# Hybrid encoder layer: first loads on two queues, both halves of the first norm together, first group's stacks without transfers, priority for copies of projection banks

## The chip, the cores and the metric

The kernel runs on one core of a Trainium2 chip. The metric is the device time of one execution in microseconds. The times of the kernel before are 1128.06, 1128.92 and 1130.89; their median, 1128.92, is the time before. The profile is of one further execution that took 1127.34.

The engines are TensorE (PE; its weight loads are PEld), VectorE (DVE), ScalarE (ACT), GpSimd (POOL) and SyncE (SP). SP and ACT issue the transfers of this kernel. A queue works its instructions in order: an instruction that waits holds all behind it on its engine.

## The reference

One encoder layer on x of 1024 tokens by 1024 channels, float32. An RMS norm feeds one projection of 2304 columns that belong to two token mixers: window attention with 8 query heads in two groups (each group of 4 shares one key and one value head, |i-j| <= 128, a sink logit per head, rotary positions on the first 16 of 64 channels), and neighbourhood attention with 8 heads on a 16 x 64 grid. Their outputs get a norm each and go through one output projection; a gated MLP of width 2816 with a convolution of width 3, and a last norm, follow.

```python
hn = rmsnorm(h, norm_mix[l])
proj = jnp.einsum('bsd,de->bse', hn, w_in[l])
qa, ka, va, qb, kb, vb = jnp.split(proj, splits, axis=-1)
qa = partial_rope(qa.reshape(B, S, A_HEADS, HEAD_DIM), cos, sin)
ka = partial_rope(ka.reshape(B, S, A_KV_HEADS, HEAD_DIM), cos, sin)
o_a = window_gqa_sink(qa, ka, va, sink[l])
o_b = neighbourhood_attention(...)
mix = jnp.concatenate([rmsnorm(o_a, norm_a[l]), rmsnorm(o_b, norm_b[l])], axis=-1)
h = h + jnp.einsum('bse,ed->bsd', mix, w_out[l])
...
h = h + conv_gated_mlp(hn, w_gate[l], w_up[l], conv_w[l], conv_b[l], w_down[l])
return rmsnorm(h, norm_final)
```

## The kernel before

Activations are held transposed: tiles of 128 channels by 1024 tokens (`S`), worked in two halves of 512 (`h`). Each float32 operand of a matmul is split in a high part (ACT, a copy to fp32r) and a low part (DVE, the difference), and a product is three matmuls: high by high, high by low, low by high (`block`, L112 to L115). One such step of three, for one 128-channel slice `k` and one half, is called a block below.

**Order.** PE's order is as written (`manual_schedule`, L91). The other engines' orders are made at build time by a scheduler that takes what is ready by priority; `tc.high_priority(offset=...)` raises the priority of what it encloses. Tiles come from pools with a fixed number of buffers by tag: `raw` 2, `whi` and `wlo` 3 each, the `s` banks of PSUM 2.

**Start (L508 to L572).** SP issues all loads: the parameters, the first half of x tile 0, the first 128 channels of the weights of projection tiles 0 and 1, the second half of x tile 0, the rest of those weights' first four slices, then x tiles 1 to 3, the weights' second halves, and x tiles 4 to 7. x tile 0 is split by halves (`first_x`), the others whole (`split_scaled`, L123). Projection tiles m = 0 (a key and a value head), 1 and 2 (two query heads each) belong to attention group 0, m = 3 to 5 to group 1, m = 6 to 17 to the grid attention. Tiles 0 and 1 run through k = 0 to 7 together as x arrives (L566 to L571). Beside it the squares of x are summed (`squares`, L135).

**First norm (L580 to L598).** The third tile's first half runs, then for each half of the tokens in turn: sums of the squares by matmuls of one column (`ss`, `inverse_narrow`, L145), a square root on ACT and a reciprocal on DVE, and a broadcast by four matmuls (`sw`, `widen`, L157), which ACT copies to `rstd1`. Then the banks of tiles 0 and 1 are copied out with the scale (`evacuate`, L168), and the third tile's second half runs, with the posts of tiles 0 and 1 among its blocks.

**Posts (L244).** `rotate` (L178) moves the rotary rows of a tile to a folded layout by two transfers issued by ACT (`f<-t`, L186), turns them in four DVE operations, and moves them back by two transfers issued by SP (`t<-f`, L192). There are two folded buffers. `split_pair` (L194) then makes from a tile of two query heads the two stacked operands `q` (high part of a head in one half of the partitions, low part in the other) by one ACT copy, one DVE operation and three transfers issued by SP (L200 to L202); `split_k` (L217) does the same for a key head with one copy, one difference and two transfers. `split_v` (L227) transposes the values on PE (`vt`).

**After that** `fill(n)` runs n blocks of the further projections and output products (`rest`, L616), each projection tile `Project.run` (L452) being 16 blocks in `pj` banks with a copy by `evacuate` after each half. `settle` (L605) calls the post of a finished tile once `LAG` blocks of the next have run. First come `FILL0` = 26 blocks; then six score steps (L710; each two matmuls into an `s` bank, L273, followed by the masked minimum `p<-s` on DVE, L295, and the exponential on ACT, L299); then `FILL1` = 12 blocks; then the units of attention, between whose steps blocks are run at `RATES`. The first two score steps use the query stacks of tile 1, the next two those of tile 2.

Of the kernel before, what the change touches and what calls it, by code (L numbers as in the profile page):

```python
# [30 lines left out]

LAG = 3
FILL0, FILL1 = 26, 12
RATES = [40, 49, 21, 21, 21, 21, 13, 19, 20, 17]
SPARE = (3, 6)
# [16 lines left out]
def hybrid_layer(tc, xT, w_in, w_out, w_gate, w_up, w_down, small, sink, rpb, consts, rope, out):  # L52
    nc = tc.nc
    with ExitStack() as ctx:
# [32 lines left out]
        cst = cpool.tile([128, K_END], F32, name="cst")  # L87
        ident = cst[:, K_ID:K_ID + 128]


# [72 lines left out]

        def inverse_rms_wide(sq, dim, tag):
            return widen(inverse_narrow([sq], dim, tag), tag)


# [10 lines left out]
        def rotate(t, n):  # L178

            m = slice(0, n)  # L180
            f, u = folded[0]
            folded.append(folded.pop(0))
            rows = lambda s: t[4 * s:n:8].rearrange("a (c w) -> a c w", w=128)
            fold = lambda s: f[m, s]
            for s in range(2):
                nc.scalar.dma_start(fold(s), rows(s))  # L186
            for s in range(2):
                nc.vector.tensor_tensor(u[m, s], f[m, 1 - s], rs[m, s], op=ALU.mult)
            nc.vector.tensor_tensor(f[m], f[m], rc[m], op=ALU.mult)
            nc.vector.tensor_tensor(f[m], f[m], u[m], op=ALU.add)  # L190
            for s in range(2):
                nc.sync.dma_start(rows(s), fold(s))  # L192

        def split_pair(t):  # L194
# [7 lines left out]
            nc.sync.dma_start(f32(a[64:128, :]), t[0:64])  # L202
            return [a, b]

        def split_qk(t):
# [239 lines left out]
        class Project:  # L445
# [64 lines left out]
        xg, first = [None] * KT, [Project(0), Project(1)]  # L510
        xts, sqs = [], []

        def load_x(k):
            xt = big("xt", "op")
            nc.sync.dma_start(xt, xT[k])
            xts.append(xt)


        xt0 = big("xt", "op")
        xts.append(xt0)  # L520
        head = [[wpool.tile([128, 4, 128], dt, name="w0", tag=tag, bufs=n) for dt, tag, n in ((F32, "raw", 2), (F32R, "whi", 3), (F32R, "wlo", 3))] for _ in first]
        nc.sync.dma_start(xt0[:, 0:HALF], xT[0, :, 0:HALF])
        for p, (raw, _, _) in zip(first, head):
            nc.sync.dma_start(raw[:, 0:1], w_in[p.m, :, 0:1, :])
        nc.sync.dma_start(xt0[:, HALF:S], xT[0, :, HALF:S])
        for p, (raw, _, _) in zip(first, head):
            nc.sync.dma_start(raw[:, 1:4], w_in[p.m, :, 1:4, :])
        xg[0] = big("xgh", "xg", F32R), big("xgl", "xg", F32R)
        g0 = col(C_NMIX)

        def first_x(h):
            nc.scalar.activation(xg[0][0][:, tsl(h)], xt0[:, tsl(h)], AF.Copy, scale=g0)
            nc.vector.scalar_tensor_tensor(xg[0][1][:, tsl(h)], xt0[:, tsl(h)], g0, f32(xg[0][0][:, tsl(h)]), op0=ALU.mult, op1=ALU.subtract)

# [11 lines left out]
        for k in range(1, 4):  # L546
            load_x(k)
        for p in first:
            p.w += load_w(w_in[p.m, :, 4:8, :])
        for k in range(4, KT):  # L550
            load_x(k)
        nc.sync.dma_start(cst, consts)
# [6 lines left out]
        nc.sync.dma_start(turns[:, 0:2], rope)  # L559
        for _ in range(2):  # L560
            t = quarters(big("f", "mix"))
            folded.append((t[:, 0], t[:, 1]))

        banks = [[bank("pj", "pj") for _ in range(2)], [bank("o", "o") for _ in range(2)]]
        acc = None
        for k in range(KT):  # L566
            if k:
                xg[k] = split_scaled(xts[k], col(C_NMIX + k), "xg", "xg")
# [784 lines left out]
```

## Time and profile before

| | |
|---|---|
| times of three runs | 1128.06, 1128.92, 1130.89 us |
| the profiled execution | 1127.34 us |
| its span | 1125.6 us |
| mean granted clock of PE | 0.984 |
| transfers | 147.03 MB |

The span runs from the first to the last instruction of the trace; the execution's own time is 1.7 us longer. In the page's first part each engine stands with its busy time, its share of the span and its instructions. A row of the waits reads: engine, operation and line, who ended the wait, total, times, longest. A row of the timeline reads: start, duration, engine, line, operation, output and inputs, shape, and in brackets the idle time before it and what ended that. The duration of an instruction that follows another closely overlaps with its neighbour's; the step from start to start is then shorter.

### The profile page before, as it was taken

The page shows a single profiled execution, that of the slowest core. Times are in us where ns is not written, and L with a number is a line of the kernel's source. Part 1 is how long each engine was busy: PE and PEld are TensorE (multiplying, and loading weights), DVE is VectorE, ACT ScalarE, POOL GpSimd, SP SyncE. Part 2 cuts the span into 40 slices and gives each one's busy share as a digit, 9 for nine tenths or more (in the row PEclk, how much of TensorE's full clock was granted, in tenths as well). Part 3 has the DMA queues.
Part 4 walks back from the last instruction along what each step waited for, and adds up shares of the span by engine and source line. Part 5 has one row for each costly group of instructions (what it writes and reads, how often), then busy time and mean ns, then how long its engine had stood idle before and what let it go on. Part 6 is the DMA issues. An engine that isn't in the chain of part 4 may idle for free.

```text
span 1125.6 us, 14912 instructions
## 1 busy us (share of the span) xinstructions
PE 1086.2 (96%) x5124; PEld 903.0 (80%) x5124; DVE 852.4 (76%) x1549; ACT 548.3 (49%) x1033; POOL 105.7 (9%) x186
## 2 busy tenths in 40 slices
PE   8969999999999999999999999999999999999995
PEld 6858888888878877888788888888888878888884
DVE  6557888766689666989988778877877868797843
ACT  7235767655667433445434334334343645543531
POOL 0212332233223100000000000000000000000001
PEclk8989999999999999999999999999999999999997
DMA  7253220333215316412443223222322799875823
GB/s 266 65 122 80 53 57 29 84 92 87 75 31 148 103 47 211 163 47 78 166 160 122 105 92 123 102 103 94 122 103 94 244 302 294 268 221 174 272 83 144
DMA packets 67708, 147.03 MB, mean 131 GB/s; under 512 B 8112, under 2 KB 16816, under 8 KB 67632
## 3 DMA queue, kind: packets, MB, share of 16 engines
q1 hardware_dynamic: 57552, 121.04, 34.6%
q10 hardware_dynamic: 10080, 25.04, 5.9%
q8 instruction: 40, 0.66, 0.2%
q14 instruction: 36, 0.29, 0.1%
HBM read 103.58 MB, written 28.57 MB: 117 GB/s over the span
## 4 chain that ended last, share of the span: by engine, by line
PE 86%; DVE 7%; DMA 3%; ACT 2%; issue 2%; SPq 0%; POOLq 0%; ACTq 0%; DVEq 0%
PE pj L113 7%; PE pj L114 7%; PE pj L115 7%; PE dn L797 6%; PE dn L799 6%; PE dn L798 6%; PE z L799 5%; PE z L797 5%; PE z L798 5%; PE x L797 3%; PE x L799 3%; PE x L798 3%; PE s L273 3%; PE y L799 3%; PE y L797 3%; PE y L798 3%
## 5 line engine op out<-in xcount | busy, mean ns | idle before, releaser
L797 PE MATMUL dn<-xd,whi 128*128 128x512 f32 x308 | 120.2, 390 | 1.1 <-ACT c L1218 1.1
L786 ACT ACTIVATE whi<-ws 128x512 fp32r<-128x512 f32 (+1 forms) x100 | 60.1, 622 | 123.9 <-DVE ws L903 76.3
L799 PE MATMUL dn<-xd,wlo 128*128 128x512 f32 x308 | 119.8, 389 | 0.0
L798 PE MATMUL dn<-xd,whi 128*128 128x512 f32 x308 | 119.8, 389 | 0.0
L799 PE MATMUL z<-hg,wlo 128*128 128x512 f32 x264 | 103.1, 390 | 0.7 <-DVE wlo L787 0.7
L113 PE MATMUL pj<-xgh,whi 128*128 128x512 f32 x248 | 103.4, 417 | 0.0
L797 PE MATMUL z<-hg,whi 128*128 128x512 f32 x264 | 102.9, 390 | 0.0
L798 PE MATMUL z<-hg,whi 128*128 128x512 f32 x264 | 102.7, 389 | 0.0
L299 ACT ACTIVATE p<-p,nm 128x385 f32<-128x385 f32 (+3 forms) x128 | 75.1, 586 | 56.3 <-DVE nm L295 52.3
L115 PE MATMUL pj<-xgh,wlo 128*128 128x512 f32 x248 | 97.7, 394 | 0.0
L114 PE MATMUL pj<-xgl,whi 128*128 128x512 f32 x248 | 97.5, 393 | 0.0
L303 POOL TENSOR_SCALAR p<-p,sm 128x384 f32<-128x384 f32 (+1 forms) x128 | 73.5, 588 | 237.3 <-DVE sm L301 218.2
L787 DVE TENSOR_TENSOR wlo<-raw,whi 128x512 fp32r<-128x512 f32 (+1 forms) x102 | 66.3, 669 | 22.7 <-ACT whi L786 22.5
L787 DVE TENSOR_TENSOR wlo<-ws,whi 128x512 fp32r<-128x512 f32 (+1 forms) x100 | 66.7, 681 | 19.5 <-ACT whi L786 19.5
L309 DVE TENSOR_TENSOR pl<-pt,ph 128x384 fp32r<-128x384 f32 (+2 forms) x108 | 63.1, 588 | 23.2 <-ACT ph L308 22.1
L786 ACT ACTIVATE whi<-raw 128x512 fp32r<-128x512 f32 (+1 forms) x102 | 60.4, 611 | 41.4 <-DMA raw<-in_w_down_dram 18.4
L1108 ACT ACTIVATE xd<-xd 128x512 fp32r<-128x512 f32 x77 | 47.3, 627 | 58.0 <-DMA xd<-x 56.5
L308 ACT ACTIVATE ph<-pt 128x384 fp32r<-128x384 f32 (+2 forms) x108 | 55.3, 514 | 38.2 <-PE pt L408 30.8
L1209 POOL TENSOR_TENSOR y<-y,wide 128x512 f32<-128x512 f32 x4 | 5.1, 1283 | 727.0 <-ACT y L1208 727.0
L799 PE MATMUL y<-hg,wlo 128*128 128x512 f32 x176 | 68.7, 390 | 0.5 <-DVE wlo L787 0.5
L797 PE MATMUL x<-hg,whi 128*128 128x512 f32 x176 | 68.7, 390 | 0.0
L799 PE MATMUL x<-hg,wlo 128*128 128x512 f32 x176 | 68.5, 389 | 0.0
(199 smaller groups left out, 2657.8 us busy)
## 6 DMA issues: line engine op xcount, KB each, us to landing
xd<-x SPq DMA_DIRECT2D x77, 256.0 KB, 5.1
raw<-in_w_down_dram SPq DMA_DIRECT2D x72, 256.0 KB, 3.4
raw<-in_w_gate_dram SPq DMA_DIRECT2D x22, 512.0 KB, 3.5
raw<-in_w_up_dram SPq DMA_DIRECT2D x22, 512.0 KB, 4.0
x<-c ACTq DMA_DIRECT2D x22, 512.0 KB
raw<-in_w_in_dram SPq DMA_DIRECT2D x32, 256.0 KB, 3.2
raw<-in_w_down_dram SPq DMA_DIRECT2D x36, 192.0 KB, 3.8
x<-t ACTq DMA_DIRECT2D x11, 512.0 KB, 2.6
```

The costliest lines, as they stand in the source:

```text
L113: nc.tensor.matmul(ps, w[0], x[0][:, tsl(h)], start=first, stop=False)
L114: nc.tensor.matmul(ps, w[0], x[1][:, tsl(h)], start=False, stop=False)
L115: nc.tensor.matmul(ps, w[1], x[0][:, tsl(h)], start=False, stop=last)
L299: nc.scalar.activation(p[:, j, 0:e], p[:, j, 0:e], AF.Exp, bias=nm, scale=-1.0, accum_out=sm[:, j:j + 1])
L303: nc.gpsimd.tensor_scalar(p[:, i, 0:m], p[:, i, 0:m], sm[:, i:i + 1], 1.0, op0=ALU.mult, op1=ALU.mult)
L308: nc.scalar.activation(ph[:, 0:n], ps[:, 0:n], AF.Copy)
L309: nc.vector.tensor_tensor(pl[:, 0:n], ps[:, 0:n], f32(ph[:, 0:n]), op=ALU.subtract)
L786: nc.scalar.activation(hi, src, AF.Copy)
L787: nc.vector.tensor_tensor(lo, src, f32(hi[:, :, :]), op=ALU.subtract)
L797: nc.tensor.matmul(ps, w[0], x[0], start=first and i == 0, stop=False, skip_group_check=True)
L798: nc.tensor.matmul(ps, w[0], x[1], start=False, stop=False, skip_group_check=True)
L799: nc.tensor.matmul(ps, w[1], x[0], start=False, stop=last and i == len(ws) - 1, skip_group_check=True)
```

## The change

- **First loads.** The parameters and the weights of tiles 0 and 1 (first four slices) are issued by ACT, ahead of its first table load. SP begins with x tiles 0 and 1, in halves; x tile 1 is now split by halves too.
- **First norm.** `ss` of both halves, three blocks of the third tile, `sw` of both halves; the other five blocks and then both posts. Those posts, and tile 2's, have a priority offset of 400.
- **Rotation.** The second `f<-t` transfer goes to SP; there is a third folded buffer.
- **First group's stacks.** `split_first` and `split_first_k` write each half of the partitions by an ACT copy and a DVE operation of 64 rows; no transfers. Group 1 keeps `split_pair` and `split_k`.
- **Numbers.** `FILL0` 26 to 22, the first two `RATES` 40, 49 to 43, 50; tile 3 is posted after `LATE` = 13 blocks in place of `LAG` = 3.
- **Bank copies** of the projection tiles (all but the last) have a priority offset of 500.

```diff
-LAG = 3
-FILL0, FILL1 = 26, 12
-RATES = [40, 49, 21, 21, 21, 21, 13, 19, 20, 17]
+LAG, LATE = 3, 13
+FILL0, FILL1 = 22, 12
+RATES = [43, 50, 21, 21, 21, 21, 13, 19, 20, 17]
...
-        nc.sync.dma_start(par[:, 0:C_SINK], small)
+        nc.scalar.dma_start(par[:, 0:C_SINK], small)
...
+        def load_x(k, parts=1):
+            xt = big("xt", "op")
+            n = S // parts
+            for i in range(parts):
+                nc.sync.dma_start(xt[:, i * n:(i + 1) * n], xT[k, :, i * n:(i + 1) * n])
+            return xt
...
+        for ks in (slice(0, 1), slice(1, 4)):
+            for m, (raw, _, _) in enumerate(head):
+                nc.scalar.dma_start(raw[:, ks], w_in[m, :, ks, :])
+        xts = [load_x(0, 2), load_x(1, 2)]
...
             for s in range(2):
-                nc.scalar.dma_start(fold(s), rows(s))
+                (nc.scalar, nc.sync)[s].dma_start(fold(s), rows(s))
...
+        def split_first(t):
+
+            a, b = big("q", "op", F32R), big("q", "op", F32R)
+            for x, hi, lo in ((a, slice(0, 64), slice(64, 128)), (b, slice(64, 128), slice(0, 64))):
+                nc.scalar.activation(x[hi], t[hi], AF.Copy, scale=-HD ** -0.5)
+                nc.vector.scalar_tensor_tensor(x[lo], t[hi], -HD ** -0.5, f32(x[hi, :]), op0=ALU.mult, op1=ALU.subtract)
+            return [a, b]
+
+        def split_first_k(t):
+            a, b = big("ka", "op", F32R), big("kb", "op", F32R)
+            up, down = slice(0, 64), slice(64, 128)
+            nc.scalar.activation(a[up], t[up], AF.Copy)
+            nc.vector.tensor_tensor(b[up], t[up], f32(a[up, :]), op=ALU.subtract)
+            nc.vector.tensor_tensor(a[down], t[up], f32(a[up, :]), op=ALU.subtract)
+            nc.scalar.activation(b[down], t[up], AF.Copy)
+            return a, b
...
-                    ka[g] = split_k(t, 0)
+                    ka[g] = split_k(t, 0) if g else split_first_k(t)
...
-                    qa[g, i - 1] = split_pair(t)
+                    qa[g, i - 1] = split_pair(t) if g else split_first(t)
...
-                        evacuate(self.t, ps, h, self.grid)
+                        with tc.high_priority(offset=500):
+                            evacuate(self.t, ps, h, self.grid)
...
-        first_x(0)
+        for k in range(2):
+            xg[k] = big("xgh", "xg", F32R), big("xgl", "xg", F32R)
+        split_x(0, 0)
         first_w(slice(0, 1))
-        first_x(1)
+        split_x(0, 1)
         first_w(slice(1, 4))
+        for h in range(2):
+            split_x(1, h)
...
-        for _ in range(2):
-            t = quarters(big("f", "mix"))
-            folded.append((t[:, 0], t[:, 1]))
+        t = quarters(big("f", "mix"))
+        folded += [(t[:, 0], t[:, 1]), (t[:, 2], t[:, 3]), (turns[:, 2], turns[:, 3])]
...
+        vs1 = [inverse_narrow([acc[:, tsl(h)]], D, "pt") for h in range(2)]
+        rest3 = product(ps3[1], third.w, xg, 1)
+        for _ in range(3):
+            next(rest3)
         for h in range(2):
-            nc.scalar.activation(rstd1[:, tsl(h)], inverse_rms_wide(acc[:, tsl(h)], D, "pt"), AF.Copy)
+            nc.scalar.activation(rstd1[:, tsl(h)], widen(vs1[h], "pt"), AF.Copy)
...
-        for i, _ in enumerate(product(ps3[1], third.w, xg, 1)):
-            if i == 3:
-                first[0].post()
-            if i == 6:
-                first[1].post()
+        for _ in rest3:
+            pass
+        for p in first:
+            with tc.high_priority(offset=400):
+                p.post()
...
-            while waiting and (len(waiting) > 1 or age >= LAG):
+            while waiting and (len(waiting) > 1 or age >= (LATE if waiting[0].m == 3 else LAG)):
...
-                waiting.pop(0).post()
+                with tc.high_priority(offset=400 if m == 2 else 0):
+                    waiting.pop(0).post()
```

More of the change, by code (lines that the diff above doesn't have):

```diff
@@ L88, in hybrid_layer @@
         ident = cst[:, K_ID:K_ID + 128]
+        def load_x(k, parts=1):
[4 more added lines that the diff above has]
+            return xt
+        head = [[wpool.tile([128, 4, 128], dt, name="w0", tag=tag, bufs=n) for dt, tag, n in ((F32, "raw", 2), (F32R, "whi", 3), (F32R, "wlo", 3))] for _ in range(2)]
+        for ks in (slice(0, 1), slice(1, 4)):
+            for m, (raw, _, _) in enumerate(head):
+                nc.scalar.dma_start(raw[:, ks], w_in[m, :, ks, :])
+        xts = [load_x(0, 2), load_x(1, 2)]
         ctx.enter_context(tc.manual_schedule(engines={mybir.EngineType.PE}))
@@ L162, in widen @@
             return wide
-        def inverse_rms_wide(sq, dim, tag):
-            return widen(inverse_narrow([sq], dim, tag), tag)
         def evacuate(t, ps, h, grid):
@@ L510, in hybrid_layer, with split_x @@
         xg, first = [None] * KT, [Project(0), Project(1)]
[L511 to L533, printed above, removed]
+        def split_x(k, h):
+            g = col(C_NMIX + k)
+            hi, lo = (t[:, tsl(h)] for t in xg[k])
+            nc.scalar.activation(hi, xts[k][:, tsl(h)], AF.Copy, scale=g)
+            nc.vector.scalar_tensor_tensor(lo, xts[k][:, tsl(h)], g, f32(hi), op0=ALU.mult, op1=ALU.subtract)
         def first_w(ks):
@@ L538, in first_w @@
                 nc.vector.tensor_tensor(lo[:, ks], raw[:, ks], f32(hi[:, ks]), op=ALU.subtract)
-        first_x(0)
+        for k in range(2):
+            xg[k] = big("xgh", "xg", F32R), big("xgl", "xg", F32R)
+        split_x(0, 0)
         first_w(slice(0, 1))
-        first_x(1)
+        split_x(0, 1)
         first_w(slice(1, 4))
+        for h in range(2):
+            split_x(1, h)
         for p, (_, hi, lo) in zip(first, head):
             p.w = [(hi[:, j, :], lo[:, j, :]) for j in range(4)]
-        for k in range(1, 4):
-            load_x(k)
+        for k in range(2, 4):
+            xts.append(load_x(k))
         for p in first:
@@ L550, in hybrid_layer @@
         for k in range(4, KT):
-            load_x(k)
+            xts.append(load_x(k))
         nc.sync.dma_start(cst, consts)
@@ L566, in hybrid_layer @@
         for k in range(KT):
-            if k:
+            if k > 1:
                 xg[k] = split_scaled(xts[k], col(C_NMIX + k), "xg", "xg")
```

## The prediction

> **What bounds the kernel now.** I read the page first, then who made PE wait, then PE's busy time in short stretches, then the order of time around the two places where PE loses most.
>
> ```profile
> span 1125.6 us, 14912 instructions
> PE 1086.2 (96%) x5124; PEld 903.0 (80%) x5124; DVE 852.4 (76%) x1549; ACT 548.3 (49%) x1033; POOL 105.7 (9%) x186
> ```
>
> PE is the bound and its order is written by hand, so only time in which PE waits or runs at a lower clock can be won: 39.4 us of idle time, and slow stretches inside the busy time. PE's waits in the first 90 us:
>
> ```profile
> PE s L273 <- DMA q<-t: 8.5, 1, 8.5
> PE pj L113 <- ACT xgh L125: 1.8, 1, 1.8
> ```
>
> The first is the score matmul that waits for the last transfer of `split_pair`; the second is the start, where the second x tile is late. Stretches of 3.41 us show what such a wait costs beside itself (the columns are length, busy time and count of PE, PEld, DVE, ACT, POOL, then granted clock, DMA share, GB/s):
>
> ```profile
> 3.80:7.21 3.41, 2.61 (x12) 1.60 (x11) 1.28 (x4) 2.00 (x5) 0.00 (x0) 1.00 0.86 249
> 7.21:10.62 3.41, 1.84 (x6) 0.94 (x6) 1.65 (x3) 2.33 (x4) 0.00 (x0) 1.00 0.90 344
> 10.62:14.04 3.42, 2.33 (x5) 1.54 (x6) 2.88 (x3) 3.42 (x5) 0.00 (x0) 0.51 0.97 355
> 14.04:17.45 3.41, 3.41 (x10) 2.64 (x9) 3.41 (x4) 3.41 (x5) 0.00 (x0) 0.50 1.00 394
> 68.65:72.06 3.41, 1.40 (x9) 1.04 (x7) 2.34 (x6) 1.62 (x2) 0.00 (x0) 1.00 0.43 96
> 72.06:75.48 3.42, 0.00 (x0) 0.00 (x0) 2.08 (x4) 2.23 (x7) 0.94 (x2) 0.51 0.42 85
> 78.89:82.30 3.41, 3.25 (x11) 2.77 (x11) 2.18 (x9) 1.71 (x7) 0.54 (x2) 0.50 0.31 94
> ```
>
> After a stretch with PE busy 1.84 or 1.40 of 3.41 the granted clock is 0.5, and it returns after one full busy stretch. Each late operand is thus paid a second time. By stage:
>
> ```profile
> 5.12:33.83 28.71, 25.97 (x96) 19.81 (x97) 23.26 (x25) 20.24 (x24) 7.24 (x7) 0.88 0.65 237
> 33.83:39.27 5.44, 5.44 (x25) 4.50 (x24) 1.81 (x3) 1.92 (x2) 0.30 (x1) 1.00 0.51 142
> 39.27:44.37 5.10, 3.78 (x34) 3.63 (x32) 1.92 (x5) 1.12 (x3) 1.58 (x4) 1.00 0.33 101
> 69.42:82.53 13.11, 4.44 (x16) 3.75 (x15) 6.36 (x18) 5.80 (x15) 1.71 (x4) 0.61 0.55 125
> 40.83 1.13 PE L161 MATMUL sw<-cst,v 128*128 128x128 f32 x8 [0.61 <-PE ss L150]
> 43.46 1.16 PE L161 MATMUL sw<-cst,v 128*128 128x128 f32 x8 [0.71 <-DVE v L154]
> ```
>
> At full clock the 24 matmuls of the third tile's first half take 5.44, 0.227 each. The 96 of the first two tiles (5.12 to 33.83) would take 21.8 and take 28.7: **6.9 lost**. The norm loses 0.61 + 0.71 = **1.3**. At the first scores PE waits 8.5 and then runs at half clock until 82.30; the 3.7 us from 78.56 on hold 1.9 of full-clock work: **10.4 lost**. In all 18.6 us lie where the change acts.
>
> **The change, part by part.** T0 is the start of the first `ss` matmul (39.27 now).
>
> *First loads.*
>
> ```profile
> 0.73 1.28 ACT L95 ACT_TABLE_LOAD   x1 [0.73 <-PEq L1342]
> 3.07 0.91 SPq L527 DMA_DIRECT2D w<-in_w_in_dram  x2
> 4.01 1.39 SPq L515 DMA_DIRECT2D xt<-in_xT_dram  x3
> 4.15 0.72 ACT L532 ACTIVATE xgh<-xt,par 128x512 fp32r<-128x512 f32 x1 [1.92 <-DMA xt<-in_xT_dram]
> 6.33 0.72 ACT L532 ACTIVATE xgh<-xt,par 128x512 fp32r<-128x512 f32 x1 [1.06 <-DMA xt<-in_xT_dram]
> 9.98 1.15 ACT L125 ACTIVATE xgh<-xt,par 128x1024 fp32r<-128x1024 f32 x1 [1.08 <-DMA xt<-in_xT_dram]
> 11.03 1.04 ACT L139 ACTIVATE sq<-xt 128x1024 f32<-128x1024 f32 x1
> 22.25 0.63 ACT L108 ACTIVATE whi<-raw 128x512 fp32r<-128x512 f32 x1 [2.65 <-PE pj L114]
> 12.36 1.22 DVE L141 TENSOR_TENSOR sq<-sq 128x1024 f32<-128x1024 f32 x1
> 13.50 1.28 DVE L126 SCALAR_TENSOR_TENSOR xgl<-xt,par,xgh 128x1024 fp32r<-128x1024 f32 x1
> ```
>
> ACT now issues five transfers (0.44 each, half of the 0.91) ahead of its table load: 0.73 + 2.2 + 1.28 + the warm-up 0.2 = 4.4 in place of 4.15, so PE starts 0.2 later. On SP the third and fourth issues are x1's halves (the fourth waits until a first transfer has landed). Its bytes gain less than the 2.4 us by which the issue is earlier, for the engines already show shares of 0.86 and 0.90 from 3.80 on; I take x1's halves at 8.4 and 9.2 instead of 9.98 (bounds: 6.33, where x0's second half is there now, and 9.98). With `split_x` per half (0.65 ACT, then 0.65 DVE) PE waits some 0.9 for k=1, and 0.5 for k=2's low part. Then something new is late: `whi` of tile 1's second weight half reuses the slot of tile 0's first. Now ACT is there early and waits 2.65 for PE. In the changed order it stands behind `xgh` of k=2 to 6, three squares and a `whi`, 5×1.05 + 3×0.95 + 0.5 (the steps of the rows 9.98 and 11.03, neighbours overlapping by 0.1) from x2's landing at 10.7, 0.52 MB at 355 GB/s after x1: 19.3; I add 0.3 for a raw weight that lands late: done at 20.2; PE, no longer slow, wants it at 18.8. With its `wlo` that stops PE 1.85. Start: 0.2 + 0.4 ramp + 0.9 + 0.5 + 1.85 = 3.9 lost in place of 6.9, **T0 = 36.3, gain 3.0**; bounds 0 (the bytes come no earlier, or the new stop costs clock) and 5.4 (only ramp and x1 remain). The third tile's operands and the squares are done by 31 by the same sums; that is cover of 5 us for the norm.
>
> By the Trainium skill ("TensorE: Matmul & The Clock Gate", section Part 1) the clock falls after an idle window of about 3.4 us; by that a stop of 1.85 costs no clock. The row 7.21:10.62 speaks against it: 1.84 busy was low enough. With the page the gain at the start stays 3.0; by the row it is 1.3 (half a stretch less) if the stop lies within one stretch.
>
> *Norm for both halves.* Both `ss`, three blocks, both `sw`, five blocks. The chain from `ss` to `v` needs 0.7 and has 2.0 us of blocks over it: the 1.3 goes, nothing is late.
>
> *Stacks without transfers.*
>
> ```profile
> 46.00 3.15 ACTq L186 DMA_DIRECT2D f<-t  x4
> 48.21 0.28 DVE L188 TENSOR_TENSOR f<-f,turns 64x128 f32<-64x128 f32 x1 [1.64 <-DMA f<-t]
> 51.61 0.41 DVE L189 TENSOR_TENSOR f<-f,turns 128x256 f32<-128x256 f32 x1
> 51.75 2.79 SPq L192 DMA_DIRECT2D t<-f  x4
> 54.58 1.06 ACT L221 ACTIVATE ka<-t 64x1024 fp32r<-64x1024 f32 x1 [4.71 <-DMA t<-f]
> 57.38 0.69 DVE L170 TENSOR_TENSOR t<-pj,rstd 128x512 f32<-128x512 f32 x1
> 59.03 0.63 ACT L108 ACTIVATE whi<-raw 128x512 fp32r<-128x512 f32 x1 [1.67 <-PE pj L114]
> 59.11 1.22 DVE L199 SCALAR_TENSOR_TENSOR t<-t,q 128x1024 fp32r<-128x1024 f32 x1
> 69.85 0.48 DVE L295 CUSTOM_DVE_ANT_0 p<-s,cst,nsink 128x256 f32<-128x256 f32 x1 [0.90 <-PE s L273]
> 74.87 0.55 SPq L202 DMA_DIRECT2D q<-t  x1
> 78.56 0.55 PE L273 MATMUL s<-ka,q 128*128 128x256 f32 x1 [8.51 <-DMA q<-t]
> ```
>
> Eight transfers go, the last issued at 74.87 and waited for until 78.56. Three 64-row ACT copies (1.06) and three DVE operations (1.22) are added; ACT and DVE have room here, but not free: they stand in one row. PE after T0: `ss` 1.9, three blocks 2.0, `sw` 2.0, five blocks 3.4, `vt` 0.8 (moved behind the blocks), third job from T0+10.1; `FILL0` is 22, so the first score comes at T0+25.1. The rotation: tiles out of the banks by T0+10.2, transfers 2.2 (48.21 from 46.00), DVE until T0+15.3, back transfers issued 0.7 apart on SP; all three tiles lie by T0+20. Two queues for `f<-t` save its serial issue. The loads that SP queues behind these transfers are for the job after next; they cost nothing.
>
> In the changed order a `whi` stands ahead of `ka` on ACT, and it waits for twelve blocks of the third job (as at 59.03), T0+18.2. Then `ka`, `kb` and four `q` copies, to T0+24.8. DVE: `kb` and `ka` low parts and one `q` (1.14 each back to back, 13.50 less 12.36), two bank copies (0.61), three `q`, a `wlo`, and the four rotation operations of job m=3 (1.3): 19.9 + 3.4 + 1.2 + 3.4 + 0.6 + 1.3 = T0+29.8. Only then stands the first `p<-s` (0.48). Score matmuls 1 and 2 fill both `s` banks at T0+25.8; the third needs the first bank back: T0+30.4. So **the wait for a transfer becomes one for DVE's queue**: 4.6, then steps 3 to 6 at DVE's pace (0.9 more), end T0+32.1. PE was idle for over half of some stretch, so the clock falls again; I charge 1.0 for what is left of it after T0+32.1 (bounds 0.2 and 1.9). Sum 6.5 in place of 10.4, **gain 3.9**; bounds 1.5 and 9.5 (`p<-s` not held).
>
> *Priority of bank copies, `LATE`, `RATES`.* The four blocks and the `vt` taken out before the scores are done later: no work is saved, and the comparison above counts losses only. m=3's stack is wanted eight units later, so posting it at 13 is free.
>
> ```profile
> 113.00:170.00 57.00, 55.82 (x305) 47.46 (x304) 48.24 (x142) 41.59 (x106) 19.19 (x43) 1.00 0.21 54
> PE vt L233 <- DVE pl L309: 2.5, 3, 1.2
> ```
>
> DVE is 85% busy there and PE loses 1.2 in 57. From 84 to 340 the transposes wait 2.5 for a bank copy that stands behind `pl`; a copy with priority could win that, and one ahead of `pl` or `p<-s` could cost its 0.69. I take +0.2; bounds -3 and +2.
>
> Sum: 3.0 + 1.3 + 3.9 + 0.2 = 8.4 of the profiled execution's 1127.34, which lies 1.6 under the median of 1128.92. Against that median: **1120.5 us**.
>
> **Rivals.**
> 1. *Both new stops are smaller*: x lands sooner, the scheduler's row on DVE runs faster than my sum. For it: PE's own wants are the only late thing. Against: the order on ACT and DVE is fixed. Gains 5.4 + 1.3 + 7.5 (10.4 less 2.9 of pacing and clock) = 14: 1115.
> 2. *The two queues bring no bytes earlier*, so the change doesn't do what it says at the start. For: shares 0.86 and 0.90, and 344 GB/s while x1 is on its way. Against: 249 GB/s before that. Gain 8.4 - 3.0 = 5.4: 1123.5. The Trainium skill ("DMA: Bandwidth & Descriptors", section Issuing engines are not separate DMA queues) says just this: all queues run on the same 16 engines, a second issuer saves issue time alone. Its time is the 1123.5; the early 249 GB/s beside a 0.86 share half agrees.
> 3. *No net change*: start 0, and the DVE row longer by two more operations that PE then waits for: gain 0 to 3, 1127.
> 4. *Slower*: bank copies with priority stand ahead of `pl` and `p<-s` in the stretch where DVE is 85% full. 28 copies at 0.69 are 19 us if PE feels each: 1139. It decides once more than 12 of 28 (8.4/0.69) hit PE. Against: one filler block (0.68) between most steps covers one copy, and in the changed order most moved ahead by one or two places.
>
> **How the numbers follow.** Forecast (1117 to 1123) 0.50; rival 1 0.17; rival 2 0.14; rival 3 0.11; rival 4 0.08. The range 1113 to 1126.5 leaves out rival 4 and part of rival 3. About 0.3%, 3.4 us, is what a measurement can tell from no change: faster 0.81, same 0.11, slower 0.08.
>
> **What would show it.** Start: PE's wait at k=1 under 1 us, clock 1.0 from 10.6 to 17.4, a new wait of `o` for ACT `whi` near 19, `ss` at 35 to 37.5. Norm: no wait before `sw`. Stacks: no `q<-t` transfer before the first scores, and PE waiting 3 to 6 us with DVE `p<-s` named; if it waits under 1, rival 1 holds. After 113: PE's idle time as now; if it grows by over 5 with DVE named, rival 4. I am wrong most likely in the DVE row before the first `p<-s`, or in when x1 lands.

## The result, and the profile after

The changed kernel takes 1118.76 us, the median of seven runs (1115.87 to 1125.44), beside 1128.39 for the kernel before (1128.06 to 1131.67): a ratio of 0.9912, 95% interval 0.9893 to 0.9932. The forecast was 1120.5. The profiled execution took 1115.87 us, the fastest of the seven, with a span of 1114.1 and a mean granted clock of 0.990.

The page of the changed kernel, its first lines:

```profile
span 1114.1 us, 14912 instructions
...
PE 1083.9 (97%) x5124; PEld 902.4 (81%) x5124; DVE 854.2 (77%) x1553; ACT 551.7 (50%) x1037; POOL 109.4 (10%) x186
```

As many instructions as before, and PE's busy time falls by only 2.3 us: what went is time in which PE stood. Where it went is read from three stages: PE's first product to the first `ss` of the first norm (T0); T0 to the end of the sixth score step; from there to the first `ss` of the second norm (`ss<-ones,sqb`, called N2 below). First the changed kernel, then the kernel before (length, busy time and count of PE, PEld, DVE, ACT, POOL, then granted clock, DMA share, GB/s).

```profile
5.47:36.10 30.63, 30.09 (x120) 23.62 (x121) 24.19 (x28) 22.32 (x27) 11.32 (x7) 1.00 0.63 225
36.10:69.22 33.12, 29.38 (x144) 24.30 (x143) 21.66 (x45) 12.14 (x18) 1.91 (x4) 0.95 0.21 63
69.22:392.09 322.87, 315.98 (x1708) 268.46 (x1708) 241.46 (x625) 207.81 (x492) 90.57 (x165) 1.00 0.28 76
```

```profile
5.12:39.27 34.15, 31.41 (x120) 24.32 (x121) 25.06 (x27) 22.16 (x26) 7.54 (x8) 0.90 0.63 222
39.27:81.56 42.29, 32.30 (x164) 27.53 (x163) 21.09 (x49) 11.78 (x23) 2.52 (x6) 0.89 0.44 106
81.56:403.35 321.79, 314.42 (x1693) 266.15 (x1692) 239.66 (x620) 205.82 (x484) 90.03 (x163) 1.00 0.28 75
```

T0 comes 3.2 earlier, the stage of norm and first scores is 9.2 shorter, and the long stage behind it is 1.1 longer. But the stages no longer hold the same work. Four blocks of 0.68 (`FILL0` 26 to 22) and the eight `vt` transposes of the fourth tile (0.8; `LATE`) moved from the second stage into the third, and one block of the output products (46 `pj<-mgh` blocks in place of 47) moved from the third to behind N2. With these counted, the second stage gained 5.7 and the third 1.8. From N2 to the end it is 722.0 after and 722.2 before. So all of the gain lies ahead of N2: 11.3 us by the mark in these two profiles, 10.6 for the same work.

PE's waits in the first 85 us of the changed kernel:

```profile
PE pj L127 <- DVE t L181: 3.1, 1, 3.1
...
PE pj L127 <- ACT w L550: 0.7, 1, 0.7
PE s L301 <- DVE nm L323: 0.6, 2, 0.4
PE o L127 <- ACT whi L122: 0.3, 1, 0.3
PE o L129 <- DVE wlo L123: 0.2, 1, 0.2
```

The waits for `q<-t`, `xgh` and `v` are gone. The largest is one that the forecast did not have: the fifth tile's first product waits 3.1 for DVE to copy the `pj` bank of the fourth tile's first half (`t`, L181). The timeline shows why it is late (ACT, then DVE, then PE):

```profile
54.24 0.63 ACT L122 ACTIVATE whi<-raw 128x512 fp32r<-128x512 f32 x1 [7.19 <-PE pj L128]
54.78 1.05 ACT L227 ACTIVATE ka<-t 64x1024 fp32r<-64x1024 f32 x1
55.85 1.06 ACT L230 ACTIVATE kb<-t 64x1024 fp32r<-64x1024 f32 x1
56.94 4.30 ACT L220 ACTIVATE q<-t 64x1024 fp32r<-64x1024 f32 x4
```

```profile
55.86 1.22 DVE L228 TENSOR_TENSOR kb<-t,ka 64x1024 fp32r<-64x1024 f32 x1 [0.26 <-ACT ka L227]
57.09 1.22 DVE L229 TENSOR_TENSOR ka<-t,ka 64x1024 fp32r<-64x1024 f32 x1
58.23 1.21 DVE L221 SCALAR_TENSOR_TENSOR q<-t,q 64x1024 fp32r<-64x1024 f32 x1
59.48 1.29 DVE L181 TENSOR_TENSOR t<-pj,rstd 128x512 f32<-128x512 f32 x2
60.80 3.72 DVE L221 SCALAR_TENSOR_TENSOR q<-t,q 64x1024 fp32r<-64x1024 f32 x3
...
66.50 0.48 DVE L323 CUSTOM_DVE_ANT_0 p<-s,cst,nsink 128x256 f32<-128x256 f32 x1
```

```profile
60.22 0.50 PE L127 MATMUL pj<-xgh,whi 128*128 128x512 f32 x1 [3.12 <-DVE t L181]
...
66.06 0.28 PE L301 MATMUL s<-ka,q 128*128 128x256 f32 x1
```

DVE's queue holds the two bank copies behind three stack operations; those wait for ACT's `ka`, and `ka` stands behind a `whi` that waits 7.19 for PE. The copy's target `t` comes from a ring of three buffers, which tiles 0 to 2 hold, so the copy cannot stand ahead of the first tile's stack. The bank was full at 51.7, where the eighth block's last matmul ends (51.28, 0.39 long). Stretches of 3.41 us around it and at the start:

```profile
57.50:60.92 3.42, 0.70 (x3) 0.61 (x4) 3.36 (x5) 3.35 (x4) 0.00 (x0) 1.00 0.03 10
60.92:64.33 3.41, 3.41 (x10) 2.66 (x9) 3.35 (x3) 0.95 (x2) 0.00 (x0) 0.51 0.08 19
```

```profile
6.30:9.72 3.42, 3.42 (x8) 2.41 (x9) 2.38 (x5) 2.97 (x6) 0.00 (x0) 1.00 0.97 329
9.72:13.13 3.41, 3.41 (x16) 2.78 (x15) 2.21 (x3) 2.74 (x3) 0.00 (x0) 1.00 1.04 396
```

The wait is paid a second time at clock 0.51. The last pair is a trap: the clock column says 1.00 in both stretches, but the first holds 8 matmuls and the second 16, all 512 wide, with PE never idle. PE ran at half speed until 9.72. The trace's first clock record begins only there, and where it has none the column prints 1.00; the durations tell the speed.

### The profile page after: what moved, and what is told of

It reads as the page before. It is cut to its first block, busy times and chain, and to the rows that moved or that the text cites. A ratio compares the mean times of both kernels' runs of the same rounds, so it can differ in the third digit from the quotient of the medians.

```text
span 1114.1 us, 14912 instructions
## 1 busy us (share of the span) xinstructions
PE 1083.9 (97%) x5124; PEld 902.4 (81%) x5124; DVE 854.2 (77%) x1553; ACT 551.7 (50%) x1037; POOL 109.4 (10%) x186
## 4 chain that ended last, share of the span: by engine, by line
PE 86%; DVE 8%; ACT 2%; issue 2%; DMA 1%; SPq 0%; POOLq 0%; POOL 0%; ACTq 0%; DVEq 0%
PE pj L127 7%; PE pj L128 7%; PE pj L129 7%; PE dn L818 6%; PE dn L820 6%; PE dn L819 6%; PE z L820 5%; PE z L818 5%; PE z L819 5%; PE x L818 3%; PE x L820 3%; PE x L819 3%; PE s L301 3%; PE y L820 3%; PE y L818 3%; PE y L819 3%
## 5 line engine op out<-in xcount | busy, mean ns | idle before, releaser
L337 DVE TENSOR_TENSOR pl<-pt,ph 128x384 fp32r<-128x384 f32 (+2 forms) x108 | 63.1, 588 | 25.6 <-ACT ph L336 24.8
L818 PEld LDWEIGHTS dn<-xd,whi 128*128 128x128 f32 x308 | 57.8, 188 | 13.5 <-ACT c L1239 1.7
```

What stands on the lines that cost most here:

```text
L337: nc.vector.tensor_tensor(pl[:, 0:n], ps[:, 0:n], f32(ph[:, 0:n]), op=ALU.subtract)
L818: nc.tensor.matmul(ps, w[0], x[0], start=first and i == 0, stop=False, skip_group_check=True)
```

## The experiments

Theory: three stops of PE were shortened (start, norm, first scores), and what is left at the first scores is the order of work on ACT's and DVE's queues. Rivals: the second queue brings nothing; the transfers of the stacks were hidden anyway; bank copies with priority cost the softmax; DVE's amount of work, not its order, sets the first scores.

A run's time moves by up to 10 us between executions of one kernel, so the marks inside the profiles carry the verdicts. Each kernel has one profile; the two of the changed kernel agree to 0.01 at the sixth step and differ by 1.1 at N2 after T0, so smaller differences at N2 say nothing. All are read from the timeline; "last stage" is from the first to the last `ss` of the norms behind N2, where all kernels have the same instructions.

| kernel | T0 | sixth step ends after T0 | N2 after T0 | last stage | median of runs, ratio to before |
|---|---|---|---|---|---|
| before | 39.27 | 42.29 | 364.08 | 657.9 | 1128.39 |
| changed | 36.10 | 33.12 | 355.99 | 657.7 | 1118.76, 0.9912 (0.9893 to 0.9932) |
| changed again | 35.65 | 33.13 | 357.10 | 662.7 | 1120.37, 0.9912 (0.9886 to 0.9937) |
| stacks by transfer | 35.74 | 36.31 | 359.76 | 657.8 | 1121.87, 0.9933 (0.9908 to 0.9957) |
| start undone | 38.91 | 33.11 | 356.10 | 660.1 | 1120.59, 0.9920 (0.9896 to 0.9945) |
| one queue, halves | 37.06 | 33.10 | 356.03 | 660.8 | 1119.02, 0.9907 (0.9883 to 0.9931) |
| copies without priority | 35.71 | 38.09 | 361.00 | 660.8 | 1122.29, 0.9932 (0.9906 to 0.9958) |
| norm by halves | 36.10 | 34.71 | 358.13 | 662.7 | 1120.31, 0.9912 (0.9889 to 0.9936) |
| before + stacks | 37.14 | 38.22 | 361.62 | 659.8 | 1122.74, 0.9943 (0.9923 to 0.9963) |
| before + priority | 39.31 | 42.31 | 364.58 | 658.8 | 1129.56, 1.0015 (0.9999 to 1.0032) |
| mended order | 35.57 | 29.31 | 352.66 | 660.4 | 1114.70, 0.9882 (0.9856 to 0.9908) |
| mended, `whi` not | 35.97 | 31.37 | 357.28 | 660.2 | 1116.77, 0.9880 (0.9860 to 0.9899) |
| mended, 25 blocks | 35.40 | 31.76 | 353.87 | 660.8 | 1115.98, 0.9876 (0.9854 to 0.9898) |
| same, squares later | 35.41 | 32.55 | 354.59 | 658.9 | 1113.88, 0.9867 (0.9844 to 0.9889) |

The rows are not all alike in the work ahead of a mark. Ahead of the sixth step's end lie 26 blocks and a second group of `vt` in the kernel before and the two made from it, 25 blocks in the last two rows and 22 in the rest; ahead of N2 these three groups have 47, 48 and 46 blocks of output products.

**The changed kernel again**, unaltered.

> The changed kernel again, unaltered, to have its profile and its spread beside the variants on one chip. Both theories: 1117 to 1121 us, ratio to the kernel before 0.990 to 0.993. If the wide spread of its runs (1115.9 to 1125.4) comes from short stops of PE that trip the half clock in some executions only, its mean granted clock falls with the time: about 0.990 in a run of 1116 and 0.985 in one of 1124; if it comes from something else, the clocks stay within 0.002.

The ratio is the same. In the first seven runs clock and time went together (0.990 at 1115.9, 0.984 at 1125.4); here the clock runs 0.987 to 0.993 and follows the time loosely (0.993 at 1116.2, but 0.990 at 1120.3), so short stops do not explain the spread alone. The two profiles of this kernel differ by 0.7 at N2 and by 5.0 in the last stage. PE's waits there, the changed kernel first, then the repeat:

```profile
PE dn L818 <- ACT c L1239: 1.3, 1, 1.3
```

```profile
PE dn L818 <- ACT c L1239: 3.6, 1, 3.6
```

Their `ss` rows (last field before the forms: first and last start):

```profile
L164 PE MATMUL ss<-ones,s x40: 164/250/271, 443.6 to 1101.3; 128*128 128x1 f32 x40
```

```profile
L164 PE MATMUL ss<-ones,s x40: 164/250/353, 444.2 to 1106.9; 128*128 128x1 f32 x40
```

On ACT the copies `c` stand behind `xd` conversions that wait for transfers `xd<-x`. This wait is 0.6 to 3.6 in the profiles here; in the repeat one stretch of 3.41 us at half clock follows it near 922. That is 2.3 + 1.7 of the 5.0. The repeat's last `ss` also run at half clock (353 ns in place of 271), which the trace grants from 1105.2 on, ahead of the mark: up to 0.8 more. In the first profile it begins at 1102.0, behind the mark. The kernel is the same, so nothing of it comes from the change.

**Stacks by transfer.**

```diff
-ka[g] = split_k(t, 0) if g else split_first_k(t)
+ka[g] = split_k(t, 0)
-qa[g, i - 1] = split_pair(t) if g else split_first(t)
+qa[g, i - 1] = split_pair(t)
```

> The changed kernel with the first group's stacks made by transfers again (the old stack functions for group 0; all else as changed, 22 blocks ahead of the first score). My theory, that these transfers end last before the first scores: the wait of the first score names the q transfer again and lasts 5 to 9 us, the sixth score step ends 4 to 8 us later after the first ss matmul than with the stacks on the engines, and the whole is 4 to 8 us slower than the changed kernel. Rival, that the row on DVE and ACT was the true limit and the transfers were hidden: within 1.5 us of the changed kernel.

PE's waits in the first 90 us of this kernel:

```profile
PE s L301 <- DMA q<-t: 4.0, 2, 3.3
PE pj L127 <- DVE t L181: 1.9, 1, 1.9
```

The sixth step ends 3.2 later after T0, N2 2.7 to 3.8. The transfers do end last again, as the theory says, but PE waits 4.0 for them and not 5 to 9, and they are worth 3.2 and not 4 to 8. With all else as changed (the posts' priority, the two queues for `f<-t`, `FILL0` 22) the last is waited for until T0+33.6 in place of T0+39.3; which of these does it was not tried. The wait for the bank copy is there too, 1.9 in place of 3.1.

**Start undone, and the second queue alone undone.** The first:

```diff
-nc.scalar.dma_start(par[:, 0:C_SINK], small)
+nc.sync.dma_start(par[:, 0:C_SINK], small)
...
-for ks in (slice(0, 1), slice(1, 4)):
+xts = [big("xt", "op")]
+for i, ks in enumerate((slice(0, 1), slice(1, 4))):
+    nc.sync.dma_start(xts[0][:, i * HALF:(i + 1) * HALF], xT[0, :, i * HALF:(i + 1) * HALF])
     for m, (raw, _, _) in enumerate(head):
-        nc.scalar.dma_start(raw[:, ks], w_in[m, :, ks, :])
-xts = [load_x(0, 2), load_x(1, 2)]
+        nc.sync.dma_start(raw[:, ks], w_in[m, :, ks, :])
+xts.append(load_x(1))
...
-for h in range(2):
-    split_x(1, h)
```

> The changed kernel with all first loads on SP's queue in the old order and the second x tile in one piece; all else as changed. My theory: the first ss matmul starts 3 us later (39.1 in place of 36.1) and the whole takes 3 us more. Rival, that two queues bring no bytes earlier: ss within 0.7 of 36.1 and the time within 1 us of the changed kernel.

The second keeps the halves: `load_x(1, 2)` behind the same loads on SP, and `split_x(1, h)`.

> The changed kernel with all first loads on SP's queue in the old order, but the second x tile still loaded and split in two halves: the second queue alone is undone. Theory 1 (the second queue is what brings x earlier): the first ss matmul near 38.5 to 39, as with both undone. Theory 2 (the halves do it, and all queues share the same engines): ss at 36 to 36.5, as in the changed kernel. In the kernels with one queue ss came at 37.1, 38.9 and 39.3 so far, with two queues at 35.6 to 36.1 in seven profiles, so 37.1 or more speaks for theory 1.

T0 is 38.91 with both undone and 37.06 with the queue alone undone; with two queues it is 35.4 to 36.1 in nine profiles. The second tile's conversion on ACT, with one queue and then in the changed kernel:

```profile
9.90 1.36 ACT L547 ACTIVATE xgh<-xt,par 128x512 fp32r<-128x512 f32 x2 [0.96 <-DMA xt<-in_xT_dram]
```

```profile
8.33 1.32 ACT L545 ACTIVATE xgh<-xt,par 128x512 fp32r<-128x512 f32 x2
```

The tile comes 1.6 earlier or more with two queues, so the rival that they bring nothing falls. At T0 the outcome lies between the two theories of the expectation: 37.06 is 1.0 to 1.7 later than with two queues, just under the 37.1 named as the sign, and it is one profile. The halves are worth between 0.1 and 2.2, for one queue and a whole tile gave T0 of 37.1, 38.9, 39.3 and 39.3. The edit also changes the order: on one queue the second tile stands behind four loads of weights. One queue with that tile ahead of the weights was not run, so the second queue and the order are not told apart. The run times cannot separate these kernels from the changed one; the 3 us expected of the whole do not show there.

**Copies without priority.** The `with tc.high_priority(offset=500):` around `evacuate` is taken out.

> The changed kernel without priority for the copies of projection banks. In its DVE row the two copies of the fourth tile's banks stand behind all four q low parts in place of behind one. Theory 1 (the wait for a bank copy sets the time of the first scores): PE's wait for that copy near 60 grows from 3.1 to 6 to 7 us, the sixth score step ends 2.5 to 4 us later, the whole 2 to 5 us slower. Theory 2 (the DVE row as a whole sets it, and its order does not matter): the wait moves but the sixth step ends within 1 us of the changed kernel, and the whole within 1.5 us. Rival 4 of the prediction (priority copies hold up the softmax later): faster by 2 us or more.

The wait, then DVE's row of this kernel:

```profile
PE pj L127 <- DVE t L181: 6.9, 1, 6.9
```

```profile
57.84 4.96 DVE L221 SCALAR_TENSOR_TENSOR q<-t,q 64x1024 fp32r<-64x1024 f32 x4
62.84 1.29 DVE L181 TENSOR_TENSOR t<-pj,rstd 128x512 f32<-128x512 f32 x2
```

Theory 1, and more than it gave: the sixth step ends 5.0 later, N2 3.9 to 5.0. Three `q` operations ahead of the copy are 3.8 of wait, and three stretches at half clock follow (59.5 to 69.7) in place of one. By run times the two kernels cannot be told apart.

**Before + priority alone**, the same `with` put into the kernel before.

> The kernel before with priority for the copies of projection banks alone. Theory (this priority is worth something only where the stacks are made on DVE, since the copies of the fourth tile stand behind no long work otherwise): the first scores and the second norm's ss within 0.7 of the kernel before, counted from the first ss (364.1 there). Rival 4 of the prediction (copies ahead of the softmax hold it up): 2 us or more longer. Additive rival: 4 us shorter, as much as the same edit is worth in the changed kernel.

```profile
39.31:81.62 42.31, 32.32 (x164) 27.52 (x163) 21.06 (x49) 11.78 (x23) 2.66 (x6) 0.93 0.44 106
```

42.31 beside 42.29, and N2 0.5 later. The same line is worth nothing without the new stacks and 4 to 5 us with them: the edits don't add up. Copies ahead of the softmax cost nothing that can be seen either way.

**Before + stacks alone.** `split_first` and `split_first_k` for group 0 in the kernel before.

> The kernel before with the new stack functions for group 0 alone (loads, norm, priorities, 26 blocks ahead of the first score all as before). With the stacks taken back out of the changed kernel the second norm's ss moved from 392.4 to 395.5, 3.1. Theory 1 (parts add up): ss of the second norm 3 us earlier than the 403.35 of the kernel before, so near 400.3. Theory 2 (without priority the bank copies of the fourth tile stand behind the new DVE work, which was worth 4.3 us in the other direction): gain 1.5 or less, 402 to 404, with a wait of PE for a bank copy of 3 us or more near 65.

Counted from T0 the sixth step comes 4.1 earlier and N2 2.5. The mark named in the expectation, 398.76, is 4.6 earlier than before, but 2.1 of that is T0, on which these functions have no part. So it lies between the two theories. No wait for a bank copy appears; PE waits 1.7 for `q` and 1.3 for the softmax instead. In this profile the clock fell at the first norm (the second `sw` group took 2.00, in the kernel before 1.16), one stretch, which takes back up to 1.7.

**Norm by halves.** `ss`, `sw` of one half, then of the other, then eight blocks, as before.

> The changed kernel with the first norm half by half again (ss, sw, ss, sw, then all eight blocks of the third tile's second half); all else as changed. My theory: sw waits 0.6 for ss and 0.7 for v as in the kernel before, and everything up to the first ss of the second norm (392.1 to 392.7 in the two profiles of the changed kernel) comes 1.3 later. Rival, that the later wait for a bank copy near 60 takes this in: that wait falls from 3.1 to about 1.8 and the second norm's ss starts within 0.4 of 392.4.

The waits of 0.6 and 0.7 are back, the wait for the bank copy stays at 3.1, and the sixth step ends 1.6 later, N2 1.0 to 2.1. The theory holds.

**The mended order.** Three things at the first scores:

```diff
-self.t = tmp("t")
+self.t = big("t3", "op") if self.m == 3 else tmp("t")
...
+if i == 0 and n == 8:
+    with tc.high_priority(offset=400), tc.issue_after(marks['copy'].ins):
+        later[0]()
+        with tc.issue_after(marks['kb'].ins):
+            jobs[2].load_rest()
+        later[1]()
+        later[2]()
```

> The changed kernel with the order ahead of the first scores mended in three places: the fourth tile lies in a buffer of another ring, so that its first bank copy needs no tile of the first three to be done; that copy stands ahead of the stacks on DVE (the second one behind them); and on ACT the weight split that waits for the third job's block 12 stands behind the two k copies. The same arithmetic. Theory (that wait is the order on two queues and a ring of three tiles, not lack of time): no wait of PE for a bank copy near 60, clock 1.0 from 36 to 70, first score near 61 in place of 66, sixth step 4 to 5 us earlier, second norm's ss at 387.5 to 389, the whole 1114 to 1116. Rival (DVE's sum of work is the limit): the wait moves to the first p<-s, gain under 1.5.

`later` holds the stacks of the first three tiles, `marks` the fourth tile's first bank copy and ACT's `kb`, `load_rest` the split of the fifth tile's second weight half; this stands in `rest`, behind the fourth tile's first half, and its second bank copy goes behind the last `q` on DVE. Without `load_rest`, so that the `whi` stays ahead of `ka`:

> As the mended order, but with the weight split left ahead of ka on ACT. Theory: ka still starts at 54.2, the six copies end near 61 and their low parts near 62.5, so the third score matmul waits 1 to 2 us; clock may stay at 1.0; second norm's ss 1 to 2 us later than with all three places mended, 389 to 390.5.

DVE of the mended order, then its stretches:

```profile
51.17 0.69 DVE L183 TENSOR_TENSOR t<-pj,rstd 128x512 f32<-128x512 f32 x1 [0.99 <-PE pj L131]
53.34 1.22 DVE L230 TENSOR_TENSOR kb<-t,ka 64x1024 fp32r<-64x1024 f32 x1 [1.49 <-ACT ka L229]
...
62.17 0.47 DVE L331 CUSTOM_DVE_ANT_0 p<-s,cst,nsink 128x256 f32<-128x256 f32 x1
```

```profile
59.46:62.87 3.41, 1.73 (x11) 1.36 (x9) 3.35 (x6) 0.47 (x1) 0.00 (x0) 1.00 0.00 0
62.87:66.29 3.42, 3.24 (x15) 2.56 (x16) 3.02 (x13) 3.28 (x9) 0.23 (x1) 1.00 0.14 35
```

The copy is done at 51.9 in place of 60, the first score comes at T0+24.9 in place of T0+30.0, the sixth step ends 3.8 earlier (4 to 5 expected) and N2 is 388.2, as the theory said; a wait of 1.7 for the first softmax row remains. With `whi` left in front that wait is 2.8, and the stretches are:

```profile
60.62:64.03 3.41, 0.90 (x6) 0.62 (x5) 3.35 (x4) 1.13 (x2) 0.00 (x0) 1.00 0.00 0
64.03:67.45 3.42, 2.95 (x9) 2.69 (x10) 2.79 (x12) 2.89 (x8) 0.00 (x0) 0.50 0.08 19
67.45:70.86 3.41, 3.41 (x9) 2.64 (x9) 1.73 (x7) 1.68 (x6) 1.00 (x3) 0.50 0.26 77
```

1.1 us more of waiting brought two stretches at half clock, and N2 came at 393.3 where 389 to 390.5 was expected, no earlier than in the changed kernel. So in this profile the two places on DVE bring nothing at N2 without the one on ACT, though the sixth step ends 1.8 earlier than in the changed kernel; the run times of the two mended kernels are the same within their intervals.

**25 blocks, and squares later.** `FILL0` 22 to 25 in the mended order; then, on top, seven ACT squares of the first norm behind the `whi` of tile 1's second weight half.

> The mended order with 25 in place of 22 blocks ahead of the first score. In the mended order the third score still waits 1.7 for the first softmax row. Theory: three blocks of 0.68 lie over that wait, it falls under 0.3, and the second norm's ss comes 1.5 earlier than the 388.2 there, counted from the first ss 351.1 in place of 352.6; the whole about 1 us faster. Rival: the blocks are then missing later between the score steps, and the total stays within 0.5.

> As the last one, and at the start seven of the eight squares on ACT behind the weight split of the second tile's second half. Theory (that split, which stands behind three squares, sets the first ss in all kernels with two queues: they come at 35.6 to 36.1 whether PE ran slow at its start or not): its row on ACT starts near 16.9 in place of 18.8 to 19.1, PE's wait of 0.3 to 0.9 for it goes, ss at 34.8 to 35.3. Rival: the squares are then late for the norm, and ss waits for them as long as was won: 35.6 to 36.1 or later.

With 25 blocks the wait for the softmax is 1.0 in place of 1.7, but a wait of 0.8 for a bank copy is new. N2 after T0 is 1.2 later, with two more output blocks (1.4) ahead of it, so for the same work nothing is won or lost: the rival holds. With the squares later, PE's waits for `whi` and `wlo` are gone, but T0 is the same. First products of the two:

```profile
5.47 0.50 PE L129 MATMUL pj<-xgh,w 128*128 128x512 f32 x1 [0.83 <-ACT w L572]
...
19.17 0.50 PE L129 MATMUL o<-xgh,whi 128*128 128x512 f32 x1 [0.53 <-ACT whi L124]
```

```profile
5.47 0.80 PE L129 MATMUL pj<-xgh,w 128*128 128x512 f32 x1 [0.70 <-ACT w L574]
```

The second began at half speed (0.80 for 0.50), and its `whi` row came at 18.4 and not at 16.9, after a wait of 0.6 for PE; whether the edit wins at full speed stays open. Its sixth step ends 0.8 later on the same two waits (0.8 and 1.0): here they fell into one stretch of 3.41 us and half clock followed, with 25 blocks alone they did not. All four mended kernels have ratios below the changed kernel's, 0.9867 to 0.9882 against 0.9912. Only the last one's interval (0.9844 to 0.9889) lies clear of the first measurement's (0.9893 to 0.9932); counted from T0, the mended order is 3.3 to 4.4 ahead of the changed kernel at N2 and 1.7 to 2.8 at the first `ss` of the next norm (441.35), where all have done the same work; it met one more stretch at half clock in between.

## Why the prediction was right, and where it was not

**Start: the sum right, its parts not.** T0 was forecast at 36.3 and is 36.10; the gain of 3.0 is 3.2. But PE did not wait 0.9 for k=1 and 0.5 for k=2. Here the half-speed start until 9.72 lay over both; yet where PE began at full speed (stacks by transfer) the wait at k=1 was only 0.2, for the tile came in time. And the stop of 1.85 for `whi` came as 0.33 and 0.22. The step behind it was right, though. ACT (the row, then PE's two):

```profile
19.14 0.62 ACT L122 ACTIVATE whi<-raw 128x512 fp32r<-128x512 f32 x1
```

```profile
19.82 0.50 PE L127 MATMUL o<-xgh,whi 128*128 128x512 f32 x1 [0.33 <-ACT whi L122]
...
20.77 0.50 PE L129 MATMUL o<-xgh,wlo 128*128 128x512 f32 x1 [0.22 <-DVE wlo L123]
```

`whi` is done at 19.8 (forecast 20.2). In profiles where PE began at full speed it waits 0.5 to 0.9 there, and T0 is still 35.4 to 36.1: ACT's row sets T0, and PE's speed ahead of it does not matter. That is why the sum held with its parts wrong.

**Rival 2 and the page on transfers.** The Trainium skill ("DMA: Bandwidth & Descriptors", section Issuing engines are not separate DMA queues) says that a second issuer saves issue time alone. Issue time is part of it here: the first half of the second tile was issued at 1.65 in place of 4.02. But the second half was issued at 4.05 in place of 4.50 (with one queue) and landed at 8.09 in place of 10.52, so 0.45 of issue goes with 2.4 of landing. That is more than the page's sentence gives; whether the second queue does it or the changed order of the loads is open, as said above.

**Norm.** 1.3 forecast; by the run that undoes it 1.6 at the sixth step, and 1.0 to 2.1 at N2.

**Stacks: the failed step is "So the wait for a transfer becomes one for DVE's queue", in its place.** The kind was right, and so were the rows: `whi` at T0+18.2 (18.14 measured), the last `q` copy at T0+24.8 (25.1), first `p<-s` at T0+29.8 (30.4). The place was not. The forecast had PE reach the first score at T0+25.1 without a stop and then wait 4.6 for an `s` bank. It counted "two bank copies (0.61)" as length of DVE's row and never asked who waits for them. PE did, 3.1, and the clock fell there; the softmax wait is then only 0.6. The mended order shows the forecast's own first score, T0+24.9, once that copy is early. The size came out near all the same because DVE's row ended where the forecast had it: the early stop took up time in which PE would have stood at the scores. In the place the forecast was wrong, and in the size it was lucky.

Sized: without waits the sixth step would end at T0+27.45 (24.92, and 4.39 less 1.86 of waits in the mended order). The changed kernel loses 5.7 there (forecast 6.5); the kernel before lost 42.29 - 27.45 - 2.72 (four blocks) - 0.8 (`vt`) - 1.3 (norm) = 10.0 (forecast 10.4, which counts on to 82.30). The gain is 4.3 in place of 3.9. It belongs to all edits that act there together: undone alone the stacks are worth 3.2, put in alone 4.1.

**Priority of bank copies: the term that was mis-sized.** +0.2 with bounds of -3 and +2, and in the changed kernel it is worth 3.9 to 5.0. The bounds came from the stretch after 113; the edit acts at 59.5, on the copy just named. Its value was inside the forecast all the same, for the row was taken from the changed order, where the copies stand behind one `q` and not four: it was booked under the stacks. Rival 4 falls: alone, the priority costs at most 0.5 at N2.

**The rest.** From the sixth step to N2 the changed kernel takes 322.9 and 324.0 in its two profiles; the kernel before, with four blocks and `vt` moved in and one output block moved out, would take 324.6. So 0.7 to 1.8 was gained there. Up to 0.4 of it is the end of the half clock in the kernel before (to 82.4); PE's waits in the stage sum to 7.3 before and 6.7 after. The wait of the transposes that the forecast hoped to win fell from 2.5 to 1.4, but one of `o` for `pl` rose from 0.3 to 1.4. Which of `LATE`, `RATES` and priority does what was not tried.

In sum 3.2 + 1.3 + 4.3 + 1.8 = 10.6 for the profiled pair, and 9.6 by the medians; the last stage's own spread of 5 is larger than the difference. The forecast gain was 8.4.

**The clock.** The Trainium skill ("TensorE: Matmul & The Clock Gate", section Part 1) has the clock fall after an idle window of some 3.4 us, in windows that run free of the kernel. The runs agree with the second part: PE's first product at the same 5.47 takes 0.50 in one profile and 0.80 in another. They differ on the first. The clock fell after stretches with PE busy 0.70 (above) and 0.90 of 3.41, and by the prediction's rows 1.40 and 1.84; it stayed after 1.73 in the mended order and 1.54 in before + priority (68.57 to 71.98). No whole idle window was needed in these runs; the border lies near half a stretch, and 1.54, 1.73 and 1.84 on the wrong sides say that busy time by the profile does not give it exactly. Nor does busy time decide alone. At the second norm of the changed kernel:

```profile
392.07:395.48 3.41, 3.41 (x33) 3.39 (x31) 1.25 (x2) 2.18 (x3) 0.00 (x0) 1.00 0.43 154
395.48:398.89 3.41, 3.41 (x11) 2.73 (x11) 0.27 (x1) 0.26 (x1) 0.00 (x0) 0.50 0.47 154
```

PE is busy throughout the first stretch, but 32 of its 33 matmuls are `ss`, of one column each, and the clock falls behind it. The same happens at this norm in 12 of the 14 profiles. So the border above is one for stretches of wide matmuls; what it is for narrow ones was not tried.

## What to carry to other kernels

When work is moved from transfers onto a vector queue, list for each instruction already in that queue who waits for it: its own length is the smaller part of its cost. An edit that is worth nothing alone can be the one that makes another pay, so undo parts in both directions, from the new kernel and onto the old one. Where run times scatter more than the effect, compare marks inside the profiles, counted from an event that the edit doesn't touch, and count what work lies ahead of each mark.

## What was not expected of the hardware

- The granted clock column showed 1.00 in a stretch in which 512-wide matmuls followed each other at half their usual rate (8 in 3.42 us, then 16 in 3.41): the trace has no clock record ahead of 9.72 there. In all 14 profiles the first record begins where PE's matmuls reach full speed, or ahead of the first of them.
- A wait of 2.8 us brought two stretches at half clock, one of 1.7 none. The first of the two had PE busy 2.95 of 3.42 and did not bring the clock back, the second, full, did. So a mended wait can be worth twice itself or just itself.
- The clock fell behind a stretch that PE had filled with matmuls of one column (3.41 of 3.41 busy). From N2 to the next norm the twelve profiles with 17 or 18 output blocks there took 49.9 with one stretch at half clock, 51.5 with two and 53.1 with three.
- One program's last 660 us, with the same instructions, took 657.7 to 662.7 in fourteen profiles; a copy behind a conversion that waits for its transfer stops PE 0.6 to 3.6 there.
